# Order of the loads in the first steps of a merge stage: branch weights and gate tiles, and rows of the output weights

## The chip, the core and the metric

The kernel runs on one core of a Trainium2 chip. The core has a matrix engine (TensorE, PE in the profile), a vector engine (VectorE, DVE), an activation engine (ScalarE, ACT), a general one (GpSimd, POOL), and SyncE (SP), which here only issues DMAs. Engines work through their own instructions in order and wait for each other by semaphores. The metric is the device time of one execution in microseconds (us).

## The reference

One layer of a diffusion transformer in float32: 2048 tokens of width 1024, and 256 context tokens. Cut to what matters here:

```
p  = h_x @ w_in                                    # k, v, q, u, vg, ga, gb
at = softmax(q k^T) v                              # 8 heads of 64: 512 columns
gm = gelu(u) * (W_s norm(gelu(vg)) + b)            # 512 columns
y  = sigmoid(ga) * (at @ w_br_attn) + sigmoid(gb) * (gm @ w_br_gm)
x  = x + g1 * (y @ w_out)
x  = x + g2 * relu(h2 @ w_ff1)^2 @ w_ff2
```

The change lies in the computation of `y`, which the kernel calls the merge.

## The kernel before

**Precision.** Each operand of a matrix product is kept as a high part (a cast to fp32r) and a low part (the difference). `split` (line 145) makes both: a cast on ScalarE (line 148) and a subtraction on VectorE (line 152). `mm3` (lines 178 to 182) multiplies in three matmuls: high by high (180), high by low (181), low by high (182), all into one PSUM bank. The pool of banks has 8 of them (line 193).

**Stages.** `project` computes all projections, `attend` the attention, unit by unit, `merge` (line 958) the branch products, gates and output projection, `ffn` the rest. Gates come to the merge as tanh of half the logits, in DRAM (`ta_d`, `tb_d`). The branch outputs are in `at_d` and `gm_d`.

**The merge.** It runs over four blocks b of 512 tokens. For each there are eight steps m, one for each 128 columns of `y`. A step takes the branch weights of these columns (tag `bw`, `br_raw` at line 932 loads them, 256 KB for each branch, and `br_weights` at line 941 splits them) and two gate tiles (tag `gt`, `gate_in` at line 950, 256 KB each). It does 24 matmuls: for the gMLP branch and then for the attention branch, four parts of the inner dimension in three matmuls each. VectorE applies a gate to each product (line 990), adds the two (line 993), and the sum is split into `y`. After the eight steps of a block, `out_mm` multiplies `y` by w_out, for each 128 tokens and each half of the columns, over the eight parts k of the inner dimension. The first of these products takes the parts 0 to 6 for both halves, and part 7 after them.

`fetch` (line 971) runs ahead: at step m it asks for the weights and gates of step m + 2. The weights of the first two steps are loaded and split during the attention, in `self.ready`. The gate tiles of these two steps are asked for right ahead of the loop (lines 977 and 978).

**Output weights.** In the first block, `load_w_out` (line 870) goes one step further at the end of each merge step. Each time it loads one of eight rows of 128 of w_out (512 KB, tag `ws`, two buffers, line 877) and splits both halves of it into `wo0` and `wo1`. Its first call also loads `g1b` (line 874), the residual gate spread over the partitions. In step m = 2 `last.sums` adds four matmuls (line 1842) and a copy on ScalarE, for the softmax sums of the last attention unit. `last.inverse` in step m = 4 turns these into reciprocals by way of DRAM.

**Memory.** Tiles of one tag share a fixed number of buffers (`SLOTS`: `gt` 6, `bw` 14, `ws` 2), and a load into a buffer waits for the last reader of what stood there. Tags of a pool get their addresses in the order in which they are first used. The pools `half`, `out` and `branch` open after the pools of the attention close, and take over their space.

**Order.** A planner puts each engine's instructions, and the DMAs of the SP queue, in an order. `order` (line 1651) fixes some stretches by hand. From the end of the first block on, all engines but SP keep the order of the program (`self.steady`, from `begin`). In the first block of the merge the planner is free, on all engines. A rule for all tags is that the first write of a tile comes after the first write of the tile of the same tag before it. So the raw weights of a step are planned after the splits of the step before.

Of the kernel before, what the change touches and what calls it, by code (L numbers as in the profile page):

```python
# [70 lines left out]
class Kern:  # L71
# [886 lines left out]
    def merge(self, first, start, last):  # L958
        nc = self.nc
        for _ in start:  # L960
            pass
        self.close("mid", "base")
        self.open("half")
        self.open("out")
        self.open("branch")
        steps = [(b, m) for b in range(NB) for m in range(KC)]
        it = iter(steps)
        q = []
        w_out = self.load_w_out()

        def fetch():
            s = next(it, None)
            if s is not None:
                q.append((self.br_weights(self.br_raw(s[1])), self.gate_in(*s)))

        inp = first
        for ws in self.ready:
            q.append((ws, self.gate_in(*next(it))))
        for b in range(NB):
            y = []  # L980
            for m in range(KC):
                fetch()
                ws, gt = q.pop(0)
                for nm in ("g", "a"):
                    ps = self.bank([TB])
                    wh, wl = ws[nm]
                    for k in range(4):
                        h, l = inp[nm][k]
                        self.mm3(ps, wh[:, k, :], wl[:, k, :], h, l, k == 0, k == 3)
                    nc.vector.scalar_tensor_tensor(  # L990
                        out=gt[nm], in0=gt[nm], scalar=1.0, in1=ps, op0=ALU.add, op1=ALU.mult
                    )
                nc.vector.tensor_tensor(out=gt["a"], in0=gt["a"], in1=gt["g"], op=ALU.add)
                yh, yl = self.sb("y", [TB], F32R), self.sb("y", [TB], F32R)
                self.split(gt["a"], yh, yl, lo_eng="dve")
                y.append((yh, yl))
                if b == 0:
                    next(w_out, None)
                    if m == 2:
                        last.sums(self.sb("raw", [TB]))  # L1000
                    if m == 4:
                        last.inverse()
            inp = {}
            if b == 0:
                begin = self.here()
            if b + 1 < NB:
                side = self.br_inputs(b + 1, inp)
            else:
                self.steady.append(range(begin, self.here()))
                self.close("branch", "pre")  # L1010
                self.open("early", side="right")
                side = self.h_early()
                next(side)
                self.last_out(y, side)
                for _ in side:
                    pass
                return
            for tt in range(TT):
                tok = slice(tt * P, (tt + 1) * P)
                xt = self.sb("xt", [D])  # L1020
                nc.sync.dma_start(xt, self.x_block(b)[tok, :])
                banks = [self.bank([512]) for _ in range(2)]

                def outer(n, ks):
                    self.out_mm(banks[n], y, tok, n, ks)

                head = KC - 1 if tt == 0 else KC
                if tt == 0:
                    for n in range(2):
                        outer(n, range(head))  # L1030
                for n in range(2):
                    cs = slice(n * 512, (n + 1) * 512)
                    ps = banks[n]
                    outer(n, range(head if tt == 0 else 0, KC))
                    part = self.sb("jk", [512])
                    nc.vector.tensor_tensor(out=part, in0=ps, in1=self.g1b[:, cs], op=ALU.mult)
                    nc.vector.tensor_tensor(out=xt[:, cs], in0=xt[:, cs], in1=part, op=ALU.add)
                    next(side, None)
                nc.sync.dma_start(self.x1_d[b][tok, :], xt)
                junk = self.sb("jk", [D], mybir.dt.bfloat16)  # L1040
                col = b * TT + tt
                nc.scalar.activation(
                    junk, xt, AF.Square, accum_out=self.ss2[:, col : col + 1]
                )
            for _ in side:
                pass
# [861 lines left out]
```

## Time and profile before

| | us |
|---|---|
| median of 3 runs | 2993.59 (2993.07 to 2994.03) |
| the profiled execution | 2993.09 |
| its span, first to last instruction | 2991.3 |
| TensorE busy | 2965.5 |
| VectorE busy | 2023.0 |
| ScalarE busy | 1355.5 |

All times in the rows of the profile are in us from the start of the span. The first merge step starts at 1395.39, the output products of the first block at 1445.20. The matmuls of the last block's merge steps end near 1706. The mean granted clock of TensorE is 0.999 of the full one over the span.

Rows of the profile name an instruction by its engine, the line of the kernel, the operation, and the tiles that it writes and reads, without their numbers. So `bw<-bw` at L148 is the cast of branch weights. `SPq` is the queue of SyncE, and its rows show when a DMA was issued. Lines 148, 152 and 180 to 182 are lines of helpers, and the names of tiles tell which work it is. In the matmuls of the first two steps the weights are called `t` (loaded during the attention), in those of later steps `bw`.

### The profile page before, as it was taken

How to read it: one execution, taken by the hardware profiler on the slowest of the kernel's cores; microseconds unless marked ns; L12 is line 12 of the kernel's file. 1: busy time of each engine (PE TensorE's matmuls, PEld its weight loads, DVE VectorE, ACT ScalarE, POOL GpSimd, SP SyncE). 2: the span in 40 equal slices, each digit the busy share in tenths (PEclk: the TensorE clock that was granted, in tenths of full speed). 3: DMA queues.
4: the chain of work that ended last, by engine and by line, in shares of the span. 5: the costliest groups of instructions: out<-in, count | busy, mean ns of one | idle time of the engine just before them, and what ended most of it. 6: DMA issues, size and time to landing. Idle time of an engine off the chain costs nothing.

```text
span 2991.3 us, 39857 instructions
## 1 busy us (share of the span) xinstructions
PE 2965.5 (99%) x14973; PEld 2301.8 (77%) x14973; DVE 2023.0 (68%) x2999; ACT 1355.5 (45%) x2058; POOL 564.9 (19%) x420
## 2 busy tenths in 40 slices
PE   7999999999999999999999999999999999999999
PEld 5888888887656565655888888888888888888887
DVE  6848567585777778886655698786656766654455
ACT  4443434342555555554322264444554344444433
POOL 0000000000788999990000000000000000000000
PEclk9999999999999999999999999999999999999999
DMA  7464646643100000012766558898676544446665
GB/s 240 121 220 122 222 141 196 181 133 109 36 12 16 12 22 20 25 33 97 242 177 183 154 186 314 310 327 305 225 241 227 183 155 155 155 149 219 208 216 204
DMA packets 330275, 485.53 MB, mean 162 GB/s; under 512 B 28953, under 2 KB 161345, under 8 KB 330082
## 3 DMA queue, kind: packets, MB, share of 16 engines
q1 hardware_dynamic: 326242, 478.40, 48.3%
q10 hardware_dynamic: 3840, 4.59, 0.4%
q8 instruction: 117, 1.92, 0.3%
q14 instruction: 76, 0.62, 0.1%
HBM read 348.56 MB, written 134.35 MB: 161 GB/s over the span
## 4 chain that ended last, share of the span: by engine, by line
PE 97%; DVE 2%; DMA 1%; SPq 0%; issue 0%; ACT 0%; ACTq 0%; DVEq 0%
PE b L1362 13%; PE b L1361 13%; PE b L1360 13%; PE b L180 11%; PE b L182 11%; PE b L181 11%; PE b L1780 9%; PE b L1800 8%; PE b L1736 2%; PE b L186 2%; DMA w<-in_w_mod 1%; PE b L1842 0%; PE b L290 0%; DVE ts L1747 0%; DVE ac L1820 0%; DVE f L1490 0%
## 5 line engine op out<-in xcount | busy, mean ns | idle before, releaser
L1467 DVE TENSOR_TENSOR f<-f,f 128x1024 fp32r<-128x1024 f32 x224 | 264.7, 1222 | 257.1 <-ACT f L1466 254.6
L1747 DVE TENSOR_REDUCE ts<-b 128x1 f32<-128x512 f32 x512 | 311.6, 682 | 105.8 <-PE b L1736 105.8
L1360 PE MATMUL b<-f,f 128*128 128x512 f32 x896 | 349.3, 390 | 0.0
L1361 PE MATMUL b<-f,f 128*128 128x512 f32 x896 | 349.0, 390 | 0.0
L1362 PE MATMUL b<-f,f 128*128 128x512 f32 x896 | 348.7, 389 | 0.0
L1466 ACT CAST f<-f 128x1024 fp32r<-128x1024 f32 x224 | 224.6, 1052 | 263.6 <-PE b L1361 255.4
L1780 PE MATMUL b<-t,t 64*128 64x512 f32 x2304 | 330.9, 400 | 0.0
L1780 PEld LDWEIGHTS b<-t,t 64*128 64x128 f32 x2304 | 226.2, 184 | 69.3 <-issue 26.0
L1823 POOL TENSOR_TENSOR ac<-ac,p 128x512 f32<-128x512 f32 x204 | 269.0, 1353 | 43.4 <-ACT p L1790 43.4
L1823 POOL TENSOR_TENSOR ac<-ac,t 128x512 f32<-128x512 f32 x146 | 233.1, 1626 | 0.0
L1790 ACT ACTIVATE p<-b 128x512 f32<-128x512 f32 x384 | 206.7, 598 | 48.3 <-PE b L1780 41.5
L152 DVE TENSOR_TENSOR w<-w,w 128x1024 fp32r<-128x1024 f32 x120 | 146.8, 1223 | 114.4 <-ACT w L148 76.3
L180 PE MATMUL b<-t,w 128*128 128x512 f32 x512 | 203.2, 397 | 0.4 <-DVE ts L1742 0.3
L182 PE MATMUL b<-t,w 128*128 128x512 f32 x512 | 199.7, 390 | 0.0
L181 PE MATMUL b<-t,w 128*128 128x512 f32 x512 | 199.5, 390 | 0.0
L1361 PEld LDWEIGHTS b<-f,f 128*128 128x128 f32 x896 | 168.2, 188 | 35.9 <-DVE f L1467 1.6
L1360 PEld LDWEIGHTS b<-f,f 128*128 128x128 f32 x896 | 168.2, 188 | 34.8
L1362 PEld LDWEIGHTS b<-f,f 128*128 128x128 f32 x896 | 168.2, 188 | 34.8
L180 PE MATMUL b<-w,t 128*128 128x512 f32 (+1 forms) x528 | 191.5, 363 | 0.2 <-DVE t L150 0.2
L148 ACT CAST w<-w 128x1024 fp32r<-128x1024 f32 x120 | 126.0, 1050 | 145.0 <-DMA w<-in_w_in 108.9
L182 PE MATMUL b<-w,t 128*128 128x512 f32 (+1 forms) x528 | 190.5, 361 | 0.1
L181 PE MATMUL b<-w,t 128*128 128x512 f32 (+1 forms) x528 | 190.1, 360 | 0.0
(261 smaller groups left out, 6120.8 us busy)
## 6 DMA issues: line engine op xcount, KB each, us to landing
w<-in_w_in SPq DMA_DIRECT2D x120, 512.0 KB
ao_d<-f SPq DMA_DIRECT2D x224, 256.0 KB
f<-ao_d SPq DMA_DIRECT2D x112, 512.0 KB
f<-w2o_d SPq DMA_DIRECT2D x112, 512.0 KB
f<-in_w_ff SPq DMA_DIRECT2D x48, 1024.0 KB
w2o_d<-f SPq DMA_DIRECT2D x112, 256.0 KB
md<-in_w_mod SPq DMA_DIRECT2D x32, 512.0 KB
f<-x_d SPq DMA_DIRECT2D x64, 256.0 KB
```

The lines of the kernel that those rows point to most:

```text
L180: mm(ps, sh, mh, start=start, stop=False, skip_group_check=skip)
L181: mm(ps, sh, ml, start=False, stop=False, skip_group_check=skip)
L182: mm(ps, sl, mh, start=False, stop=stop, skip_group_check=skip)
L1360: mm(ps, wh, hh, start=start and k == 0, stop=False, skip_group_check=True)
L1361: mm(ps, wh, hl, start=False, stop=False, skip_group_check=True)
L1362: mm(ps, wl, hh, start=False, stop=k == len(w) - 1, skip_group_check=True)
L1466: self.nc.scalar.copy(h, f32(l))
L1467: self.nc.vector.tensor_tensor(out=l, in0=f32(l), in1=f32(h), op=ALU.subtract)
L1747: nc.vector.tensor_reduce(out=self.mx[:, t, h, c : c + 1], in_=ps[h], axis=AX.X, op=ALU.max)
L1780: self.nc.tensor.matmul(ps[h], keys[h], q[rows[h]], start=n == 0, stop=n == len(steps) - 1, skip_group_check=True,)
L1800: nc.tensor.matmul(self.o[h * HD : (h + 1) * HD, :], k.V[c][:, i, self.kv * HD : (self.kv + 1) * HD], pt[h], start=j == 0, stop=j == NKT - 1,)
L1823: nc.gpsimd.tensor_tensor(out=self.acc[e][:, h], in0=old[:, h], in1=pt[h], op=ALU.add)
```

## The change

Three edits in `merge`. The raw weights of steps 2 and 3 are asked for in the loop that asks for the gates of steps 0 and 1, one set ahead of each pair of gates. `fetch` uses these raw weights where there are some, and still splits them at steps 0 and 1. The rows of w_out move from the end of a step to the place after the fetch of the next one. Steps 1 to 7 then take one row each, and the last row is taken after the loop, where the end of step 7 was.

```diff
         def fetch():
             s = next(it, None)
             if s is not None:
-                q.append((self.br_weights(self.br_raw(s[1])), self.gate_in(*s)))
+                raw = raws.pop(0) if raws else self.br_raw(s[1])
+                q.append((self.br_weights(raw), self.gate_in(*s)))
 
         inp = first
-        for ws in self.ready:
+        raws = []
+        for n, ws in enumerate(self.ready):
+            raws.append(self.br_raw(steps[len(self.ready) + n][1]))
             q.append((ws, self.gate_in(*next(it))))
         for b in range(NB):
             y = []
             for m in range(KC):
                 fetch()
                 ws, gt = q.pop(0)
+                if b == 0 and m:
+                    next(w_out, None)
                 for nm in ("g", "a"):
...
                 y.append((yh, yl))
                 if b == 0:
-                    next(w_out, None)
                     if m == 2:
                         last.sums(self.sb("raw", [TB]))
                     if m == 4:
                         last.inverse()
             inp = {}
             if b == 0:
+                next(w_out, None)
                 begin = self.here()
```

## The prediction

> **What bounds the kernel now.** I read the page first, for the engines and the chain.
>
> ```profile
> span 2991.3 us, 39857 instructions
> PE 2965.5 (99%) x14973; PEld 2301.8 (77%) x14973; DVE 2023.0 (68%) x2999; ACT 1355.5 (45%) x2058; POOL 564.9 (19%) x420
> ...
> PE 97%; DVE 2%; DMA 1%; SPq 0%; issue 0%; ACT 0%; ACTq 0%; DVEq 0%
> ```
>
> TensorE is busy for 2965.5 of 2991.3 us. The change adds and removes no matmul, so it can only touch what is left: 25.8 us of gaps, and any stretch in which matmuls run slowly. The waits of TensorE over the whole span say where the gaps are (columns: sum in us, times, longest).
>
> ```profile
> PE b L290 <- DMA w<-in_w_mod: 11.4, 5, 9.9
> ...
> PE b L182 <- DVE bw L152: 2.4, 1, 2.4
> PE b L1360 <- ACT f L1317: 0.7, 1, 0.7
> ...
> PE b L186 <- DVE f L1113: 0.6, 1, 0.6
> ```
>
> Only the row at L182 belongs to the stage that is edited: once, a matmul waits for the low half of branch weights (bw). It stands at the third merge step (m = 2), in TensorE's timeline. Columns: start, duration, instruction, and in brackets the idle time before it.
>
> ```profile
> 1406.41 0.40 PE L182 MATMUL b<-in,t 128*128 128x512 f32 x1
> 1406.86 0.50 PE L180 MATMUL b<-in,bw 128*128 128x512 f32 x1
> 1407.20 0.39 PE L181 MATMUL b<-in,bw 128*128 128x512 f32 x1
> 1410.00 0.50 PE L182 MATMUL b<-in,bw 128*128 128x512 f32 x1 [2.41 <-DVE bw L152]
> ...
> 1416.54 0.39 PE L182 MATMUL b<-in,bw 128*128 128x512 f32 x1
> 1416.86 1.08 PE L1842 MATMUL b<-raw,ones 128*64 128x512 f32 x4
> ...
> 1423.44 0.39 PE L180 MATMUL b<-in,bw 128*128 128x512 f32 x1
> ...
> 1428.88 0.39 PE L180 MATMUL b<-in,bw 128*128 128x512 f32 x1
> ```
>
> A step has 24 matmuls. An undisturbed one, m = 4, lasts from 1423.44 to 1428.88, that is 5.44 us, 0.23 us a matmul. Step m = 1 ends with the matmul at 1406.41, so m = 2 could start at 1406.64 and be done at 1412.08. The next thing after it, the sums at L1842, starts at 1416.86. The step costs about **4.7 us** too much, after 0.1 us for the switch to the sums. The wait explains only 2.4 us of this; the granted clock explains most of the rest. In the rows of stretches each engine has its busy us, and the third number from the end is the clock (PEclk), before the DMA share and GB/s.
>
> ```profile
> 1405.00:1407.00 2.00, 1.95 (x9) 1.27 (x8) 0.15 (x1) 0.81 (x2) 0.00 (x0) 1.00 1.05 378
> 1407.00:1410.00 3.00, 0.59 (x3) 0.16 (x3) 3.00 (x6) 0.95 (x2) 0.00 (x0) 1.00 0.94 344
> 1411.00:1412.00 1.00, 1.00 (x3) 0.72 (x3) 0.14 (x1) 0.88 (x2) 0.00 (x0) 0.50 1.11 394
> 1413.00:1414.00 1.00, 1.00 (x4) 0.81 (x3) 0.04 (x1) 0.43 (x1) 0.00 (x0) 0.50 1.05 396
> 1415.00:1416.00 1.00, 1.00 (x6) 0.82 (x5) 1.00 (x3) 0.00 (x0) 0.00 (x0) 1.00 1.11 386
> ```
>
> After the wait the clock is 0.50 in the stretches from 1411 to 1414 and full again by 1415. The DMA share is about 1 throughout: loads limit this start. Their order is in the timeline of the SP queue, and what they release in those of VectorE and ScalarE.
>
> ```profile
> 1399.24 0.34 SPq L954 DMA_DIRECT2D gt<-ta_d  x1
> ...
> 1401.05 0.43 SPq L938 DMA_DIRECT2D bw<-in_w_br_attn  x1
> 1401.53 0.51 SPq L938 DMA_DIRECT2D bw<-in_w_br_gm  x1
> ...
> 1403.63 0.38 SPq L877 DMA_DIRECT2D ws<-in_w_out  x1
> ```
>
> ```profile
> 1401.93 1.44 DVE L990 SCALAR_TENSOR_TENSOR gt<-gt,b 128x512 f32<-128x512 f32 x2 [1.51 <-DMA gt<-ta_d]
> 1406.19 1.14 ACT L148 CAST bw<-bw 128x512 fp32r<-128x512 f32 x2 [1.38 <-DMA bw<-in_w_br_gm]
> 1406.85 1.29 DVE L990 SCALAR_TENSOR_TENSOR gt<-gt,b 128x512 f32<-128x512 f32 x2 [2.75 <-PE b L182]
> 1408.05 0.69 DVE L152 TENSOR_TENSOR y<-gt,y 128x512 fp32r<-128x512 f32 x1
> 1408.65 0.68 DVE L993 TENSOR_TENSOR gt<-gt,gt 128x512 f32<-128x512 f32 x1
> 1409.26 1.29 DVE L152 TENSOR_TENSOR bw<-bw,bw 128x512 fp32r<-128x512 f32 x2
> ```
>
> The weights of m = 2 are the fifth and sixth load asked for. They are there at 1406.19, 0.45 us before TensorE wants them. The cast takes 0.6 us, and the subtraction stands in VectorE's queue behind four operations on gate tiles, until 1409.26.
>
> **The change part by part.** *Weights first.* The new order at the start is the two weight loads of m = 2, the gates of m = 0, the weights of m = 3, the gates of m = 1. No transfer is added: eight DMAs of 256 KB trade places, and those of m = 3 jump the gates of m = 1 and 2, the g1 broadcast and the first row of w_out. The first load landed at 1401.93 and the sixth at 1406.19, so 4.26/5 = 0.85 us per load (estimate). By that the weights of m = 2 are in at 1402.8, the gates of m = 0 at 1404.5, the weights of m = 3 at 1406.2, the gates of m = 1 at 1407.9. One cast and two subtractions (0.6 + 1.29 us) put the low halves of m = 2 at about 1404.7. The first is wanted as third matmul, 1406.64 + 0.45 = 1407.1. Margin 2.4 us, so the wait goes: **-4.7 us**, with its slow stretch. Weights of m = 3 then have from 1406.2 to 1413.2 (1412.08 and 1.1 us of sums). What is late next is the gate work of m = 0, at about 1404.5 for 1401.93. It holds only PSUM banks: the kernel has 8, a step uses two in 5.44 us, and two steps' worth are released by 1409, so TensorE doesn't feel it; without that cover it would cost the 2.6 us.
>
> *Rows of w_out behind each step's loads.* A row now stands behind one more set of weights and gates, four loads of 256 KB, 4 x 0.85 = 3.4 us at the rate above. Its cast and subtraction stand behind the weights' ones. The last row keeps its place after the loop. The seventh row is what TensorE needs first:
>
> ```profile
> 1442.35 1.30 DVE L152 TENSOR_TENSOR wo<-ws,wo 128x512 fp32r<-128x512 f32 x2 [0.40 <-ACT wo L148]
> ...
> 1449.28 0.39 PE L180 MATMUL b<-wo,y 128*128 128x512 f32 x1
> ```
>
> Its low half was ready at 1443.04, and the matmuls on it start at 1449.28, with the low half in the second, 1449.5. Of 6.5 us slack the 4.7 that TensorE gains go, and 1.8 stay: with nothing else moved, the row is late by 0 to 1.6 us. I take 0, since the SP queue's loads of these steps wait for gate tiles that TensorE's own steps release; they move up with it, and the DMA had room then (one row of the SP queue's waits, and a stretch with a DMA share of 0.76):
>
> ```profile
> SPq L954 <- DVE gt L993: 21.2, 10, 3.2
> ```
>
> ```profile
> 1420.00:1425.00 5.00, 5.00 (x23) 4.14 (x23) 4.60 (x9) 3.26 (x7) 0.00 (x0) 1.00 0.76 252
> ```
>
> *Tiles that change places.* In the pool called branch, memory goes by first use, so weights and gates trade places. The loads at L1106 that later reuse that space then follow the last reader of other tiles. Today the first starts at 1709.34, after the last gate tile is read at 1708.62, while bw was last read at 1706.1 (first row, of that tile's readers); TensorE waits 0.6 us for their scaling (row L186 <- DVE f L1113 above). I take half, **-0.3 us**, ends 0 and -0.6.
>
> ```profile
> L182 PE MATMUL b<-in,bw x240: 387/389/628, 1410.0 to 1706.1; 128*128 128x512 f32 x120
> ```
>
> ```profile
> 1708.62 0.69 DVE L152 TENSOR_TENSOR y<-gt,y 128x512 fp32r<-128x512 f32 x1 [0.69 <-ACT y L148]
> ...
> 1709.34 11.54 SPq L1106 DMA_DIRECT2D f<-x_d  x14
> ```
>
> *Sum.* The profiled execution took 2993.09 us, 0.5 below the median of 2993.59; 1.8 us lie outside its span. -4.7 - 0.3 = -5.0: 2988.1 in such an execution, 2988.6 as a median.
>
> A rule to weigh. The Trainium skill, "TensorE: Matmul & The Clock Gate", Part 1, says that the clock halves after an idle window of about 3.4 us, in windows that run freely. The row shows 0.50 after only 2.41 us of wait, so the measurement goes against the length; that only 1.00 and 0.50 appear agrees. By the rule alone this wait would cost no clock, and its removal would bring 2.4 us and not 4.7.
>
> **The rivals.**
>
> *The wait moves to later steps, in part.* VectorE is nearly full here (4.60 of 5.00 us from 1420 on, above), and the low halves of the later steps were barely in time:
>
> ```profile
> 1420.76 0.68 DVE L152 TENSOR_TENSOR bw<-bw,bw 128x512 fp32r<-128x512 f32 x1
> ...
> 1433.11 0.68 DVE L152 TENSOR_TENSOR bw<-bw,bw 128x512 fp32r<-128x512 f32 x1
> ...
> 1439.45 0.69 DVE L152 TENSOR_TENSOR bw<-bw,bw 128x512 fp32r<-128x512 f32 x1
> ```
>
> m = 4 has its first low half at 1421.44, for a matmul at 1423.44 + 0.45: 2.5 us to spare. m = 6 starts at 1428.88 + 5.44 = 1434.32 and has 1433.79 for 1434.77: 1.0 us. m = 7 starts at 1439.76 and has 1440.14 for 1440.21: 0.1 us. The margin shrinks because VectorE catches up on what it lost at the start. With TensorE 4.7 us ahead, these splits must move up as well. Against: two splits of m = 3 leave this crowded stretch for the early idle time of VectorE (2.75 us in the row at 1406.85). If half of the gain is given back: 2993.59 - 2.5 = 2991.1.
>
> *It moves there entirely: slower.* If the splits stay where they are in time, m = 4 is late by 4.7 - 2.5 = 2.2 us and m = 7 by 4.6 in all, over four steps. One wait of 2.2 us is like the one removed (2.41) and could bring the slow stretch again, at 4.7 - 2.4 = 2.3 us: -4.7 + 4.6 + 2.3 = +2.2, 2995.8. A late seventh row would act alike. It decides from the point where the low half of m = 4 comes after 1419.2 (1423.44 + 0.45 - 4.7). For it: nothing is taken from VectorE's total. Against: gates and sums of m = 2 hang on TensorE and come earlier.
>
> *The wait stays.* If the operations on gates, now fed later, still stand ahead of the subtraction, it waits for gates at 1404.5 and 1407.9 and TensorE for it: 0 to -2 us, 2992.6. Against: the weights land first.
>
> *The clock doesn't follow.* Were the slow stretch not a consequence of the wait but of its own timing, only the waits go: 2993.59 - 2.4 = 2991.2.
>
> *More than forecast.* If the earlier loads at L1106 also ease VectorE before the 0.7 us wait at L1360: -4.7 - 0.6 - 0.7 = -6.0, 2987.6.
>
> **How the numbers follow.** Forecast 0.60; half given back 0.19; slower 0.07; wait stays 0.05; clock doesn't follow 0.03; more 0.06. The forecast's own range is 2987.9 to 2989.2: its small term, and 0.5 us between executions. For 8 in 10 I go from 2987.4 to 2993.0, which leaves out the slower case and the edges of the two beside it. About 0.2%, 6.0 us, is what a measurement of this kernel can tell from no change, and the whole gain known is 4.7 + 0.6 us. So within 0.2% takes the forecast and nearly all rivals, 0.90; faster 0.07, from the last rival; slower 0.03, from a second slow stretch in the slower one.
>
> **What would show it.** Right: no wait of TensorE on bw at L182, clock 1.00 from 1400 on, the step m = 2 in 5.4 us, the first load at L938 at about 1399.2, casts of bw before the first operation at L990. Wrong: waits of TensorE at L180 to L182 on bw or wo between 1413 and 1450, a clock of 0.50 there, or a first load that starts later than 1399.2 since its space comes free later.

## The result, and the profile after

The changed kernel takes **2990.35 us** (median of 22 runs, 2988.38 to 2992.05). The kernel before took 2994.10 beside it (22 runs, 2991.99 to 2997.19). The ratio is 0.9987, with a 95% interval of 0.9981 to 0.9993. That is 3.75 us, 0.13%: a small gain, clear of zero, but within the 0.2% that the forecast counted as no change. The forecast was 2988.6, with 2987.9 to 2989.2 for its own case and 2987.4 to 2993.0 for 8 in 10. The measured median lies in the wide range and above the narrow one, and 3.75 of the 5.0 us that were forecast came. The profiled execution took 2989.96 us.

The head of the page says that the same 14973 matmuls are done in a span that is 3.1 us shorter.

```profile
span 2988.2 us, 39855 instructions
PE 2964.9 (99%) x14973; PEld 2301.4 (77%) x14973; DVE 2021.9 (68%) x2999; ACT 1355.0 (45%) x2058; POOL 564.4 (19%) x420
```

In the waits of TensorE over the whole span (sum, times, longest), the rows for `bw` and for `L186 <- DVE f` are gone. (The view leaves out waits shorter than about 0.2 us.) Behind the stage, those of the last stage remain (L1365 was L1360 before the edit).

```profile
PE b L290 <- DMA w<-in_w_mod: 11.1, 4, 9.9
PE b L260 <- DMA t<-in_b_mod: 3.6, 1, 3.6
PE b L1365 <- ACT f L1322: 0.7, 1, 0.7
...
PE b L1365 <- DVE f L1375: 0.7, 2, 0.4
```

In TensorE's timeline, step m = 2 starts at 1407.23 without a gap. The stretches behind it have a clock of 1.00 (third number from the end), where before it was 0.50 from 1411 to 1414.

```profile
1406.99 0.40 PE L182 MATMUL b<-in,t 128*128 128x512 f32 x1
1407.23 0.39 PE L180 MATMUL b<-in,bw 128*128 128x512 f32 x1
1407.45 0.39 PE L181 MATMUL b<-in,bw 128*128 128x512 f32 x1
1407.68 0.39 PE L182 MATMUL b<-in,bw 128*128 128x512 f32 x1
```

```profile
1407.00:1410.00 3.00, 3.00 (x15) 2.49 (x14) 3.00 (x6) 1.67 (x3) 0.00 (x0) 1.00 0.92 342
1411.00:1412.00 1.00, 1.00 (x7) 0.81 (x6) 1.00 (x3) 0.00 (x0) 0.00 (x0) 1.00 0.85 170
1413.00:1414.00 1.00, 1.00 (x5) 0.23 (x2) 0.92 (x2) 0.72 (x2) 0.00 (x0) 1.00 0.82 209
```

I lined up the two profiled executions matmul by matmul. Over step m = 2 the new one gains 4.68 us (forecast 4.7): 3.03 by the wait and the matmuls right behind it, 1.65 in the stretch at half clock. It loses 0.43 in step m = 4, gains 0.84 at the first scaling of the last stage (forecast 0.3), and loses 0.58 before the merge and about 1.4 in the feed-forward part, where nothing was edited and where other pairs of executions differ by as much. The sum is a gain of 3.1.

ScalarE's and VectorE's timelines show what makes the weights ready now. The second column is the duration, and the brackets hold the idle time before.

```profile
1403.88 1.14 ACT L148 CAST bw<-bw 128x512 fp32r<-128x512 f32 x2 [7.18 <-DMA bw<-in_w_br_gm]
```

```profile
1405.66 0.69 DVE L995 SCALAR_TENSOR_TENSOR gt<-gt,b 128x512 f32<-128x512 f32 x1 [4.66 <-DMA gt<-ta_d]
1406.26 0.68 DVE L152 TENSOR_TENSOR bw<-bw,bw 128x512 fp32r<-128x512 f32 x1
1406.87 0.68 DVE L995 SCALAR_TENSOR_TENSOR gt<-gt,b 128x512 f32<-128x512 f32 x1
1407.46 0.68 DVE L152 TENSOR_TENSOR bw<-bw,bw 128x512 fp32r<-128x512 f32 x1
```

The cast was done by 1404.5, but VectorE then waited for a gate tile until 1405.66, because a gate operation stands ahead of the subtraction in its queue. The low half was ready at 1406.94 for a matmul at 1407.68. That margin is 0.74 us, not the 2.4 of the forecast. The gate work of m = 0 came 1.2 us later than forecast, 0.6 of it since all ran later, and TensorE did not wait for it, as forecast.

### The profile page after: what moved, and what is told of

Same layout as the page of the kernel before. It is cut to its first block, busy times and chain, and to the rows that moved or that the text cites. A ratio compares the mean times of both kernels' runs of the same rounds, so it can differ in the third digit from the quotient of the medians.

```text
span 2988.2 us, 39855 instructions
## 1 busy us (share of the span) xinstructions
PE 2964.9 (99%) x14973; PEld 2301.4 (77%) x14973; DVE 2021.9 (68%) x2999; ACT 1355.0 (45%) x2058; POOL 564.4 (19%) x420
## 5 line engine op out<-in xcount | busy, mean ns | idle before, releaser
L1365 PE MATMUL b<-f,f 128*128 128x512 f32 x896 | 349.3, 390 | 0.0
L1365 PEld LDWEIGHTS b<-f,f 128*128 128x128 f32 x896 | 168.2, 188 | 34.7
```

The costliest lines, as they stand in the source:

```text
L1365: mm(ps, wh, hh, start=start and k == 0, stop=False, skip_group_check=True)
```

## The experiments

Diffs are against the changed kernel, but for the last one. "Waits" are those of TensorE from 1380 to 1460, if nothing else is said.

### One part at a time

**Weights first, without the move of the rows.**

```diff
-                if b == 0 and m:
-                    next(w_out, None)
                 for nm in ("g", "a"):
...
                 if b == 0:
+                    next(w_out, None)
                     if m == 2:
...
             if b == 0:
-                next(w_out, None)
                 begin = self.here()
```

> The weights of m = 2 and 3 come first, but rows of w_out stay at the end of each step, ahead of the next step's loads. Theory (loads land in the order asked for, and the row move protects the weights of m = 4): the loss of 4.7 us at m = 2 is gone, but TensorE waits at m = 4 by 0.3 us as in the changed kernel and by about 1.7 us more (one more row of 512 KB ahead of these weights), 2.0 us, perhaps with a stretch at clock 0.50: 1.7 to 4 us slower than the changed kernel. Rival (the wait at m = 4 comes from VectorE's queue alone, the row move does nothing): the wait at m = 4 stays at 0.3 us or less and the time is that of the changed kernel within 0.5 us.

Measured: 2989.56 us (11 runs), ratio 0.9985 (0.9976 to 0.9994) to the kernel before, which took 2994.41 beside it. Behind the attention the profile has these waits and no others:

```profile
PE b L1363 <- ACT f L1320: 0.7, 1, 0.7
PE b L1363 <- DVE f L1373: 0.3, 1, 0.3
PE b L1365 <- DVE f L1291: 0.2, 1, 0.2
```

No matmul of the merge has a wait that the view lists, at m = 4 either. So the moved rows are not needed to avoid such a wait, and this half alone brings 4.85 us. Shorter delays are there, and are counted below.

**Only the rows moved.**

```diff
         for n, ws in enumerate(self.ready):
-            raws.append(self.br_raw(steps[len(self.ready) + n][1]))
             q.append((ws, self.gate_in(*next(it))))
```

> Only the rows of w_out move; the weights of m = 2 and 3 stay behind the gates of m = 0 and 1. Theory: TensorE waits 2 to 2.5 us at m = 2 as before, and a stretch at clock 0.50 of about 3.4 us follows; time that of the kernel before within 1 us. Rival (the row move brings part of the gain): the time is 1 us or more below the kernel before, or the wait at m = 2 is under 1.5 us.

Measured: 2997.55 us, ratio 1.0010 (1.0001 to 1.0019): 3.1 us slower than before. TensorE's waits, and the SP queue (issue time, duration):

```profile
PE b L182 <- DVE bw L152: 2.6, 2, 2.2
PE b L180 <- ACT bw L148: 0.9, 2, 0.7
```

```profile
1405.47 0.32 SPq L954 DMA_DIRECT2D gt<-ta_d  x1
1409.95 0.32 SPq L954 DMA_DIRECT2D gt<-tb_d  x1
1410.32 0.43 SPq L938 DMA_DIRECT2D bw<-in_w_br_attn  x1
1410.80 0.50 SPq L938 DMA_DIRECT2D bw<-in_w_br_gm  x1
```

The wait at m = 2 stays, and new ones come at m = 6 and m = 7 (0.69 and 0.40 us). Lined up with the first profile before, steps m = 5 to 7 lose 2.0 us; the rest of the 3.1 has no place in the merge. One difference is in the queue. Before, the weights of m = 3 were asked for at 1404.05 (L938) ahead of two gate loads. Here they stand behind a gate load that waits for a free gate buffer until 1409.95, and go out 6.3 us later, of which 1.2 come from a later end of the attention. In the changed kernel they have left before. That this delay makes the waits at m = 6 and 7 is not shown. ScalarE's timeline has the cast that TensorE waits for at m = 6:

```profile
1435.48 0.62 ACT L148 CAST bw<-bw 128x512 fp32r<-128x512 f32 x1 [3.91 <-PE b L182]
```

By this row the cast itself waited for a matmul, and not for its load. The two edits are not independent, by the times: alone the move of the rows costs 3.1 us, and added to weights first it changes the median by 0.75 (below).

**The tiles' old places in memory, with the new order.**

```diff
-    def gate_in(self, b, m):
+    def gate_in(self, b, m, tiles=None):
...
-            gt = self.sb("gt", [TB])
+            gt = tiles.pop(0) if tiles else self.sb("gt", [TB])
...
         for n, ws in enumerate(self.ready):
+            tiles = [self.sb("gt", [TB]) for _ in range(2)]
             raws.append(self.br_raw(steps[len(self.ready) + n][1]))
-            q.append((ws, self.gate_in(*next(it))))
+            q.append((ws, self.gate_in(*next(it), tiles)))
```

> The changed kernel with the gate tiles named first, so that tags gt and bw have the addresses of before; every engine's order is that of the changed kernel. Theory (the changed kernel gains 0.6 to 0.8 us in the last block since the loads of the feed-forward input reuse space of bw instead of gt): the wait of 0.6 us of TensorE on the scaling (L186) is back, and the first of these loads starts after the last gate tile is read; 0.6 to 0.8 us slower than the changed kernel. Rival (addresses do nothing, the difference was chance): no such wait, same time within 0.3 us.

Measured: 2990.26 us, ratio 0.9988 (0.9979 to 0.9997). The wait at the last stage's first scaling is back, and with 1.3 us it is longer than the 0.6 expected. In TensorE's waits from 1460 on:

```profile
PE b L186 <- DVE f L1119: 1.3, 1, 1.3
```

The first load into this space starts at 1705.12, just after the last gate tile is read (1704.40 and 0.69 us); in the changed kernel it starts at 1697.2. The other profiles agree: the wait, of 0.4 to 1.3 us, is in all six in which the gate tiles come first in memory, and in none of the seven in which the weights do. So the trade of places is the cause that this wait went. VectorE's timelines show it too, here of the kernel before and of the changed one: the first scaling moved from 1715.63, behind a wait for its load, to 1708.61.

```profile
1715.63 2.29 DVE L1113 TENSOR_TENSOR f<-f,fs 128x2048 f32<-128x2048 f32 x1 [3.38 <-DMA f<-x_d]
```

```profile
1708.61 2.29 DVE L1118 TENSOR_TENSOR f<-f,fs 128x2048 f32<-128x2048 f32 x1
```

What it is worth in the median is open: in time this kernel stands between the others of its batch, in which the changed kernel did not run.

**The g1 broadcast at the fifth row.** It looked as if this load, which comes between the gates in the changed kernel, made the 0.43 us at m = 4.

```diff
         self.wo = []
-        self.g1b = self.sb("g1", [D])
-        nc.sync.dma_start(self.g1b, self.g1_d.partition_broadcast(P)[:, 0, :])
         for k in range(KC):
+            if k == 4:
+                self.g1b = self.sb("g1", [D])
+                nc.sync.dma_start(self.g1b, self.g1_d.partition_broadcast(P)[:, 0, :])
```

> The changed kernel with the broadcast of g1 (512 KB) asked for with the fifth row of w_out instead of ahead of the first. Theory (the new wait of 0.3 us at m = 4 is there because the weights of m = 4 land late, behind g1 and the first row): the weights of m = 4 are cast 1 us or more earlier relative to their step, the wait is gone, 0.3 to 0.5 us faster than the changed kernel. Rival (VectorE's queue is what is late): the wait at m = 4 stays at 0.3 us or moves to another step, same time within 0.3 us.

Measured: 2991.08 us, ratio 0.9988 (0.9979 to 0.9997). No wait at m = 4, but three on late rows of w_out:

```profile
PE b L180 <- ACT wo L148: 1.1, 1, 1.1
PE b L181 <- DVE wo L152: 0.4, 2, 0.2
```

The wait of 1.1 us and one of 0.2 are on the seventh row, the late row that the forecast had bounded at 1.6 us. It comes when the 512 KB are asked for between the fourth and the fifth row and not ahead of the first: the seventh row goes out at 1442.11, in the changed kernel at 1437.78. The expected gain of 0.3 to 0.5 us did not come. This kernel is 3.3 us below the one before, the changed kernel 3.75 to 4.40 in its three batches.

### Does the half clock always follow the wait?

**The kernel before, twice more, for its clock.** No edit.

> The kernel before once more. Theory (the clock is granted in windows of 3.4 us that run freely, and a window that is mostly idle halves the next one): TensorE waits 2.2 to 2.6 us at m = 2 again, but the slow stretch depends on where the window's edges fall: if the wait lies in one window a stretch of 3.4 us at clock 0.50 follows and the step m = 2 costs about 4.7 us too much; if an edge cuts it, there is no slow stretch and it costs 2.4 to 2.9 us. Rival (the stretch belongs to the wait whatever the time): always a stretch of about 3.4 us.

> As b1_before_again: the wait at m = 2 is 2.2 to 2.6 us; by the theory the slow stretch is there or not by the place of the wait among windows of 3.4 us counted from the first rise of the clock, by the rival it is always there.

Measured: 2994.81 and 2992.59 us. The waits of the two, first execution and then second:

```profile
PE b L182 <- DVE bw L152: 2.0, 1, 2.0
PE b L180 <- ACT bw L148: 0.5, 1, 0.5
```

```profile
PE b L182 <- DVE bw L152: 2.0, 1, 2.0
PE b L180 <- ACT bw L148: 0.4, 1, 0.4
```

They wait alike, but the stretches, in the same order, do not run alike:

```profile
1411.00:1412.00 1.00, 1.00 (x4) 0.79 (x3) 0.15 (x1) 1.00 (x2) 0.00 (x0) 0.50 1.10 388
```

```profile
1411.00:1412.00 1.00, 1.00 (x6) 0.83 (x5) 0.58 (x1) 0.80 (x2) 0.00 (x0) 1.00 1.15 380
```

The same wait brings the half clock in one execution and not in the other. Lined up, the second execution is 1.65 us shorter over this step than the profiled one of the forecast, close to half of 3.41 us. The records of the clock say why. A change to 0.50 always comes a whole number of windows of 3.413 us after the first full clock (408 windows in four executions; in the first profile from 18.25 to 1410.89), and lasts one or two windows. The change to 0.50 that ends every execution lies on the same grid. Counted on that grid, the idle time of TensorE in the window before the change, or in the fullest window, was:

| execution | window with most idle time | idle in it, us | clock behind it |
|---|---|---|---|
| before, profiled first | 1407.48 to 1410.89 | 2.41 | 0.50 for 3.41 us |
| before, second | 1406.33 to 1409.75 | 2.21 | 0.50 for 3.41 us |
| rows moved only | 1407.47 to 1410.89 | 2.17 | 0.50 for 3.41 us |
| before, third | 1406.00 to 1409.41 | 1.44 | 1.00 |

A window of the first repeat with 1.46 us of idle time, in the feed-forward part, brought no half clock either. So the wait must fall mostly into one window, and the phase of the windows differs from run to run. The mean clock of each timed run of the kernel before bears it out. In three batches it was 0.999 in 60 of 81 runs, with a median of 2994.47, and 1.000 in 21, with a median of 2992.54. It was 1.000 in 42 of 44 runs of the changed kernel. The reading is rounded and includes up to 2.6 us at 0.50 at the end of the span (the most in a profile), so single runs may be sorted wrongly. The stretch costs about 1.7 us in some three quarters of the runs.

**The changed kernel and weights first alone, side by side in two batches.** No further edit.

> The changed kernel once more. Theory (the wait of 0.3 us at m = 4 and the waits of 0.3 to 0.4 us in the feed-forward part are chance, from how loads land in an execution): no wait over 0.2 us at m = 4, no wait of TensorE in the last block's merge on the scaling; 4 to 5 us below the kernel before. Rival (these waits belong to the new order): the wait at m = 4 is there again with 0.2 to 0.5 us, and the kernel is 0.3 us or more slower than the one with the weights alone.

> Weights first, rows of w_out as before, once more and beside the changed kernel. Theory (moving the rows does nothing once the weights come first): within 0.5 us of the changed kernel, no wait at m = 2 to 7. Rival (the row move costs, as it does alone): 0.6 us or more faster than the changed kernel.

> The changed kernel, beside the one with the weights first alone. If the moved rows of the output weights cost nothing, as forecast, the two agree within 0.4 us, and no wait on weights between 1400 and 1450. If the rows cost something (the 0.43 us at m = 4 in one execution), this one is 0.5 to 1 us slower.

> Weights first, rows of the output weights at their old place. As said for the changed kernel beside it: the same within 0.4 us, or 0.5 to 1 us faster; about 4.5 us below the kernel before in either case.

Measured, 11 runs each, beside the kernel before at 2993.86 and 2993.87:

| batch | changed kernel | weights first alone |
|---|---|---|
| second | 2989.74, ratio 0.9986 (0.9977 to 0.9994) | 2989.03, 0.9983 (0.9974 to 0.9992) |
| third | 2989.47, ratio 0.9985 (0.9977 to 0.9994) | 2988.83, 0.9984 (0.9975 to 0.9993) |

In none of the four profiles does a matmul of the merge have a wait that the view lists, so the 0.43 us at m = 4 is no fixed part of the changed kernel. Over both batches its median is 0.75 us higher; drawing again from the 22 and 22 times gives 0.2 to 1.8. In each batch alone that interval includes zero (-0.5 to 1.7, and -0.6 to 2.7).

The profiles speak the other way. From the start of m = 2 to the first output product, undisturbed steps add up to 33.88 us. The changed kernel took 34.31, 33.88 and 33.91 us in its three profiles, weights first alone 34.01, 34.61 and 34.39. So with the rows at their old place steps m = 4 to 7 lose 0.1 to 0.7 us in short delays, and with the rows moved they lose 0 to 0.4. The output products of the first block took 19.95 us in all six. Whether the moved rows cost anything is open: if they do, it is not in the merge.

### How many loads ahead?

**One pair of gate tiles ahead of the weights.**

```diff
         for n, ws in enumerate(self.ready):
-            raws.append(self.br_raw(steps[len(self.ready) + n][1]))
             q.append((ws, self.gate_in(*next(it))))
+            raws.append(self.br_raw(steps[len(self.ready) + n][1]))
```

> The changed kernel with the gate tiles of m = 0 asked for ahead of the weights of m = 2 again (two loads of 256 KB), those of m = 1 still behind them. The operations are the same. If only the place in the load queue decides (2 x 0.85 us later, margin 0.74), TensorE waits 1.0 us at the first low half of m = 2. If VectorE's queue decides (there the subtraction stands behind the gate work of m = 0 and one operation of m = 1), the wait is 0 to 0.5 us. In both the wait is under 1.5 us, so by the theory that the clock halves only after more than about 2 us of idling in one window of 3.41 us, no stretch at half clock: 0 to 1.0 us above the changed kernel, and a spread of the times like that kernel's. By the rival, in which any wait here brings the stretch, 2 to 3 us above it.

Measured: 2991.58 us, 2.1 above the changed kernel beside it (0.1 to 2.9, drawing again from the 11 and 11 times); ratio to before 0.9992 (0.9983 to 1.0001); clock 1.000 in all 11 runs. The wait is 0.93 us. Its cause is in the rows of ScalarE, VectorE and TensorE:

```profile
1406.43 1.14 ACT L148 CAST bw<-bw 128x512 fp32r<-128x512 f32 x2
```

```profile
1408.48 0.69 DVE L995 SCALAR_TENSOR_TENSOR gt<-gt,b 128x512 f32<-128x512 f32 x1 [1.38 <-PE b L182]
1409.08 0.69 DVE L152 TENSOR_TENSOR bw<-bw,bw 128x512 fp32r<-128x512 f32 x1
```

```profile
1408.04 0.40 PE L182 MATMUL b<-in,t 128*128 128x512 f32 x1
...
1409.82 0.50 PE L182 MATMUL b<-in,bw 128*128 128x512 f32 x1 [0.93 <-DVE bw L152]
1410.16 0.40 PE L180 MATMUL b<-in,bw 128*128 128x512 f32 x1
```

The first cast was done by about 1407.05, and VectorE stood idle for 1.38 us with the subtraction next but one. Ahead of it in the queue was a gate operation of m = 1, which can't start before the last matmul of m = 1 (1408.04 to 1408.44). Then come 0.6 us for it and 0.69 for the subtraction, and the matmul starts at 1409.82. The number fits the expectation by the place among the loads (1.0), but the rows show that VectorE's queue sets it, and my 0 to 0.5 for that was too small. A short wait without half clock fits the windows. Lined up with the changed kernel's profile of this batch, the step at m = 2 takes 1.27 us more, and the first scaling (which waits 0.4 again, since gates come first in memory) 0.64. Together that is 1.9 of the 2.1 us. A wait costs about 0.3 us more than the view lists. Matmuls that follow each other start 0.23 us apart though the rows give each 0.39, and a wait is counted from the end of the one before; and the first one behind it takes 0.34 to the next (1409.82 to 1410.16).

**A row of w_out ahead of everything**, an edit of the kernel before:

```diff
         inp = first
+        next(w_out, None)
         for ws in self.ready:
```

> The kernel before with the g1 broadcast and the first row of the output weights (two loads of 512 KB) ahead of everything else: the weights of m = 2 land about 4 x 0.85 = 3.4 us later and the wait grows from 2.4 to 4 to 6.5 us. By the theory of the windows, a wait that long covers more than two thirds of one window in whatever phase, so the clock is 0.50 for 3.41 us after it in every execution: 3.4 us or more over the kernel before. By the rival, that the half clock is a matter of its own timing and not of the idle time, it may be absent.

Measured: 2998.89 us in one execution, 5.0 above the median before beside it. TensorE waits 4.05 us for the cast at m = 2, and 0.4 at m = 7:

```profile
PE b L180 <- ACT bw L148: 4.0, 1, 4.0
PE b L182 <- DVE bw L152: 0.4, 1, 0.4
```

```profile
1411.00:1412.00 1.00, 1.00 (x3) 0.69 (x4) 1.00 (x2) 0.24 (x1) 0.00 (x0) 0.50 0.98 357
1413.00:1415.00 2.00, 2.00 (x6) 1.54 (x5) 1.71 (x3) 1.10 (x3) 0.00 (x0) 0.50 0.98 305
1415.00:1417.00 2.00, 2.00 (x6) 1.57 (x6) 0.71 (x2) 0.86 (x2) 0.00 (x0) 0.58 1.01 369
```

The half clock follows as expected, but for two windows, 6.83 us, and not one. The window before it had 3.1 us of idle time, and the first slow window 0.9 us. This is one execution, with one place of the wait among the windows: an edge in the middle of 4.05 us would leave 2.0 us in each, so "in every execution" is not shown.

## Why the prediction was right, and where it was off

**The step at m = 2.** Forecast -4.7 in the profiled execution, measured -4.68. As a median it was mis-sized. The loss is 3.0 us of waiting (in the third execution before: 0.42 and 2.03 listed, and the matmuls that refill the pipeline) plus 1.7 us of half clock, and the second part comes in about three of four runs: 3.0 + 0.74 x 1.7 = 4.3. The forecast took one execution with the slow stretch for the rule. The Trainium skill, "TensorE: Matmul & The Clock Gate", Part 1, has a window that runs freely, of 4096 cycles, about 3.4 us, and says that the cold state comes after an idle window of that length. The length and the free running agree with the 3.413 us here. That the window must be idle throughout does not: 2.17 us of idle time in it were enough, 1.44 were not. The forecast weighed the length of the wait against this rule, and passed over its words on the phase, from which one could have worked out that the loss is not there in every run.

**Why the wait went.** The forecast's reason was that the loads land first. The estimate of the landing held: the cast started at 1403.88, and with 0.6 us by which the attention ran later the forecast has 1403.4. But the wait before was for the most part not a wait for a load. The matmul of m = 1 ended at 1406.8, and four gate operations and the subtraction followed at 0.6 us each, which ends at 1410.0, when TensorE went on. The trial with one pair ahead shows the same chain with one gate operation: 0.93 us. The load had a smaller share: in the two repeats of the kernel before, TensorE first waits 0.5 and 0.4 us for the cast, which starts when its load is there (ScalarE, first repeat):

```profile
1406.64 1.14 ACT L148 CAST bw<-bw 128x512 fp32r<-128x512 f32 x2 [1.93 <-DMA bw<-in_w_br_gm]
```

With the subtraction right behind the cast, the low half would have been ready 0.4 to 0.9 us late in the three executions (an estimate from the end of the first cast and 0.69 us). The wait went because, with the weights asked for first, the planner put the subtraction ahead of the gate work of m = 1. The rival "wait stays" had named this order, with 0.05, and was half right: a gate operation of m = 0 does stand ahead, and leaves a margin of 0.74 us.

**Rows of w_out.** Forecast 0, with 0 to 1.6 as ends. The seventh row was in time: its low half was ready at 1445.16, 0.7 us before the matmul that reads it, where the forecast had counted from 1.8 us to spare to 1.6 too late. The median is 0.75 us higher (0.2 to 1.8) than without the move, but the merge is not longer in the profiles, so this cost stays open. Alone, the move costs 3.1 us.

**Tiles that change places.** Forecast -0.3, ends 0 and -0.6. Measured -0.84 in the pair of profiled executions, and 0.93 and 0.59 against the two repeats of the kernel before: the wait goes wholly, not by half, and the matmuls behind it gain too.

**The sum.** Weights first with the trade of places should bring 4.3 + 0.8 = 5.1 in the median, less the 0.1 to 0.7 of short delays, and three batches measured 4.85, 4.83 and 5.04 for it alone. So the forecast of 5.0 fits this half, in part by luck: the step was 0.4 too large as a median and the places in memory 0.5 too small, and the two cancel. The changed kernel should bring 4.7 to 5.1 by the same sum, and brought 3.75, 4.12 and 4.40 in three batches. Where the difference goes is not shown. The range of 8 in 10 held because it was wide; the narrow one did not.

**The rivals.** The wait moved in part, to m = 4, in one of three profiles, by 0.43 us; not to the four steps that the rival priced. The point that the forecast had named for it, a low half of m = 4 after 1419.2, is 1419.8 with the 0.6 us by which all ran later, and the low half came at 1420.05. "The clock doesn't follow" is true of about one run in four. The slower case came about nowhere: the kernel with the moved rows alone is slower, with waits at m = 6 and 7, but it keeps the wait at m = 2, and its slow stretch is the one behind that wait. "More than forecast" did not come either, since the wait of 0.7 us at L1360 stays (L1365 in the changed kernel).

## What to carry to other kernels

Before you move a load, read the queue of the engine that makes its data usable: the wait for a weight was above all a place behind four gate operations, and the load order mattered since it changed that place. Test the parts of an edit one by one, also when the whole gains: here one half alone brings 4.8 to 5.0 us, and for the other no gain in time could be shown. When a view lists no wait, still compare how long the steps take: short delays added up to 0.7 us. Where a short wait brings a slow clock, count in how many runs it does, before you book its cost in full.

## What was not expected of the hardware

The granted clock changes only on a grid of 3.413 us that starts with the first full clock and is not tied to the program's work. Three windows with 2.17 to 2.41 us of idle TensorE were each followed by a window at half clock, windows with 1.44 and 1.46 us were not. After 4.05 us of waiting the half clock lasted two windows: TensorE was idle for 0.9 us of the first. In the three executions where the half clock lasted one window, TensorE was idle for 0 to 0.3 us of it. How much idle time in a slow window keeps the clock low these runs don't tell. A cost of this kind shows in the times as two groups: 2992.54 and 2994.47 us for the same kernel.
